# A two-block transformer with a 16,384-expert layer on one core: low halves on VectorE, the query left running, a bf16 key lookup

## The chip, the core and the metric

The program runs on one core of a Trainium2 chip. That core has TensorE (PE, whose weight loads are listed as PEld), VectorE (DVE), ScalarE (ACT), GpSimd (POOL) and a queue engine SP, all of which take their instructions strictly in order and wait for each other through semaphores. The metric is the device time of one execution in microseconds, the median of several runs, lower being better. Beside the runs there is one execution taken with the hardware profiler. All times in this text are from that execution, counted from the start of its span, unless a run is named.

## The reference

Two transformer blocks run over 512 tokens of width 1024. The change touches the last part of the second one, a layer that picks 128 experts per token (8 heads with 16 each) out of 16,384 by product keys:

```python
def block(hb):                                   # 128 tokens at a time
    qry = rms_norm((hb @ w_query).reshape(128, 8, 256), query_gain)
    s1 = einsum("thd,nd->thn", qry[..., :128], sub_keys_1)
    s2 = einsum("thd,nd->thn", qry[..., 128:], sub_keys_2)
    v1, i1 = top_k(s1, 16); v2, i2 = top_k(s2, 16)
    cand_s = (v1[..., :, None] + v2[..., None, :]).reshape(128, 8, 256)
    cand_i = (i1[..., :, None] * 128 + i2[..., None, :]).reshape(128, 8, 256)
    top_s, pos = top_k(cand_s, 16)
    experts = take_along_axis(cand_i, pos, -1)
    gates = softmax(top_s, -1)
    act = gelu(einsum("thkd,td->thk", expert_down[experts], hb))
    return einsum("thk,thkd->td", gates * act, expert_up[experts])
```

## The kernel before

Tokens lie in four tiles of 128. For tiles 1 to 3 (384 tokens) the kernel computes all 16,384 experts densely, in 128 blocks of 128 experts. A *down* of one block is 24 matmuls into a tile `dn` (L394 to L396) and a GELU on ACT; an *up* is 18 matmuls (L2030 to L2032) that add into six PSUM banks. Between the two the result is multiplied by the gate of each expert and token, which is zero for experts not chosen. For tile 0 the chosen rows are fetched from HBM by indirect DMA, 128 *down* rows and then 128 *up* rows (`gather_tile`), and DVE does one multiplication of 1024 columns for each of them (`row`, L1905, and `yacc`, L1914).

Every fp32 matmul is made of three: weights are split into a high half `whi` (ACT, L318) and a *low half* `wlo` = `raw` - `whi` (L328). The splits are made per *unit* of 128x1024 weights, which is one down or one up block, and `ws_at` keeps three units in flight. Which engine makes a low half is said by `lo_pool(u)`.

The expert layer has these stages, in program order:
- the query: 16 projections on PE, for each of 8 heads a score matmul against the keys and four rounds of `top16` (pairs of token tiles) on DVE (`query_scores`);
- the table (`NPRE` = 74 downs, whose results go to HBM). Beside them DVE makes the *choice* of each tile (`choose`: order 1, 0, 2, 3), which ends with a lookup of the chosen keys by comparing, multiplying and reducing (L1863 to L1868), and for tiles 1, 2 and 3 the *build* of the gate table (`w_build`): three PE transposes of keys and gates (L1939), then 32 steps of DVE one-hots and products (L1956, L1957, L1961) with 8 small matmuls each (L1972);
- the pairs: 54 downs, each followed by the up of the block before;
- the ups: the 74 stored blocks, 75 ups in all. For each, DVE makes `acte` (L2010, L2011), ACT `chi`, DVE `clo` (L2015); then one low half and one gather row at most.

What stands where in the engines' streams is decided while the program is written out. Generators in lanes are advanced by a clock `now` that each PE group moves forward; `room(cost)` holds a generator back while the DVE load that it has been told of (`self.dve`) is ahead of that clock. The lines of the change are in `lo_pool`, `ws_lo`, `query_scores`, `choose`, `w_build` and `peer`.

Of the kernel before, what the change touches and what calls it, by code (L numbers as in the profile page):

```python
# [23 lines left out]
P = 128  # L24
# [60 lines left out]
LO_POOL = 72  # L85
# [181 lines left out]
class Emit:  # L267
# [17 lines left out]
    def ws_open(self):  # L285

        self.units = [self.a["ws"][u] for u in range(len(self.seq) // 8)]
        self.first_expert = len(self.units)
        dn = lambda b: self.a["dn"][b]
        up = lambda b: self.a["up"][b * P:(b + 1) * P]  # L290
        for b in range(NPRE):
            self.units.append(dn(b))
        for b in range(NPRE, NB):
            self.units.append(dn(b))
            if b > NPRE:
                self.units.append(up(b - 1))
# [6 lines left out]
        self.u_dma = self.u_hi = self.u_lo = 0  # L303

# [17 lines left out]
    def ws_lo(self, upto):  # L322
        while self.u_lo < min(upto, self.NU):
            u = self.u_lo
            self.ws_hi(u + 1)
            l = self.wp.tile([P, D], F32R, tag="wlo", name=self.uid("wlo"), bufs=3)
            e = self.nc.gpsimd if self.lo_pool(u) else self.nc.vector
            e.tensor_tensor(l, self.raw.pop(u), self.hi[u].bitcast(F32), op=OP.subtract)  # L328
            self.lo[u] = l
            self.u_lo += 1  # L330

    def lo_pool(self, u):

        first = self.first_expert
        return u in self.pool_units or first - 16 <= u < first + LO_POOL or u >= first + NPRE and u % 3 == 0
# [1384 lines left out]
    def query_scores(self):  # L1720

        nc, v = self.nc, self.nc.vector
        keys = self.fp.tile([P, 2, P], F32, name="keys")
# [3 lines left out]
        def score(h, qg, q):  # L1727
            yield Q_Y
            qss = self.mmt("bg", (P, TT))
            self.sumsq(qss, q, True, True)  # L1730
            yield 0.4
            r = self.fwork((P, TT), tag="qr", bufs=2)
            v.tensor_scalar(r, qss, 1.0 / 256, EPS, op0=OP.mult, op1=OP.add)
            nc.gpsimd.tensor_tensor(r, r, self.mhalf.to_broadcast([P, TT]), op=OP.pow)
            for f in range(2):
                ps = self.mmt("bg", (P, TT, P))
                for t in range(TT):
                    nc.tensor.matmul(ps[:, t], lhsT=qg[f][:, t * P:(t + 1) * P], rhs=keys[:, f], start=True, stop=True)
                yield 0.4
                w = self.fwork((P, TT, P), tag="score_r", bufs=1)  # L1740
# [6 lines left out]
                v.tensor_tensor(val, val, r[:, :, None].to_broadcast([P, TT, 16]), op=OP.mult)  # L1747

        def head(h, ps):
            qg, q = [], []  # L1750
            for f in range(2):
                a = self.fwork(tag="qs", bufs=4)
                nc.scalar.activation(a, ps[f], AF.Square)
                q.append(a)
                g = self.fwork(tag="qg", bufs=4)
                nc.scalar.activation(g, ps[f], AF.Copy, scale=self.col("pq_gain", f))
                qg.append(g)
# [17 lines left out]
        self.drain()  # L1775
# [16 lines left out]
    def choose(self, t):  # L1792
# [45 lines left out]
        def blend(o, m, other):  # L1838
            v.tensor_tensor(other, other, o, op=OP.subtract)
            v.tensor_tensor(other, other, m, op=OP.mult)  # L1840
            v.tensor_tensor(o, o, other, op=OP.add)

        shifted(a, OP.logical_shift_right, 4)
# [5 lines left out]
        blend(a, mc, pf)  # L1849
# [5 lines left out]
        v.tensor_tensor(b, b, mc, op=OP.mult)  # L1855
        for f, sel in ((0, a), (1, b)):
            ix = s16("ch_ix")
            v.tensor_copy(ix, self.idx[f][:, t].bitcast(I32))
            for h0 in range(0, H, 4):
                hs = slice(h0, h0 + 4)  # L1860
                yield from self.room(1.2)
                oh = self.fwork((P, 4, 16, 16), tag="ch_oh", bufs=1)
                v.tensor_tensor(oh, sel[:, hs, :, None].to_broadcast([P, 4, 16, 16]),  # L1863
                                self.iota[:, None, None, :16].to_broadcast([P, 4, 16, 16]), op=OP.is_equal)
                yield from self.room(1.2)
                v.tensor_tensor(oh, oh, ix[:, hs, None, :].to_broadcast([P, 4, 16, 16]), op=OP.mult)
                yield from self.room(1.2)
                v.tensor_reduce(self.key[f][:, t, hs], oh, axis=mybir.AxisListType.X, op=OP.add)  # L1868
# [61 lines left out]
    def w_build(self, t):  # L1930
# [10 lines left out]
        sel = self.fwork((P, 4, P), F16, tag="sel")  # L1941
        nc.scalar.copy(sel[:, 0:2], ps[:, 0:2])
        nc.scalar.activation(sel[:, 2], ps[:, 2], AF.Copy, scale=G_UP)
        yield 0.8
        v.scalar_tensor_tensor(sel[:, 3], ps[:, 2], G_UP, sel[:, 2], op0=OP.mult, op1=OP.subtract)
# [6 lines left out]
        for j in range(P // 4 + 1):  # L1952
            if j < P // 4:
# [6 lines left out]
                for q in range(2):  # L1960
                    v.tensor_tensor(w[j % 2][:, q], one1, at(2 + q), op=OP.mult)  # L1961
# [89 lines left out]
    def peer(self):  # L2051
        nc, v = self.nc, self.nc.vector
        self.iota = self.fp.tile([P, P], F32, name="iota")
        nc.gpsimd.iota(self.iota, pattern=[[1, P]], base=0, channel_multiplier=0, allow_small_or_imprecise_dtypes=True)
        self.iota2 = self.fp.tile([P, P, 2], F16, name="iota2")
# [6 lines left out]
        ps = self.tok_major([[q.bitcast(F32) for q, _ in self.h], [q.bitcast(F32) for _, q in self.h]], 0)  # L2062
        for b in range(2):
            c = slice(b * T, (b + 1) * T)
            nc.scalar.copy(h2[:, c], ps[b])
            v.tensor_tensor(h2[:, c], h2[:, c], ps[2 + b], op=OP.add)
        self.chosen = set()
        self.built = set()
        self.dve = self.now
        self.dumping = False  # L2070
        lane = Lane()

        self.start_lane(lane)

        def chooses():
            for i, t in enumerate(CH_ORDER):
# [4 lines left out]
        lane.append(chooses())  # L2081
        for t in range(G0, TT):
            self.bg.append(self.w_build(t))
# [5 lines left out]
        self.gather_dt = G_DT  # L2089
        self.bg2.append(gather())  # L2090

        u = self.first_expert
        self.bp = self.fp
        kept = ExitStack()
        self.stage = kept.enter_context(self.tc.tile_pool(name="kept", bufs=1)).tile([P, P, P], F32, name="stage")
        with self.phase("table", 1):
            for b in range(NPRE):
# [181 lines left out]
```

## Time and profile before

| | us |
|---|---|
| median of 3 runs (3250.32 to 3255.26) | 3254.34 |
| the profiled execution: its time | 3259.43 |
| its span, first to last instruction | 3256.7 |
| PE busy, of the span | 3079.3 (95%) |
| DVE busy | 2298.4 (71%) |
| POOL busy | 991.7 (30%) |
| low halves on DVE, 364 of them, busy | 447.1 |
| low halves on POOL, 174 of them, busy | 466.1 |

The span is what the profile's rows are counted in. The execution's own time is 2.7 us longer, for what lies around the span, and 5.1 us above the median of the runs. Busy shares are averages over stages with different limits, so the stages are to be read one by one.

### The profile page before, as it was taken

Reading aid. Unit: us, or ns where it says so; the run is one execution under the profiler, and the core shown is the slowest. Engines: PE = TensorE matmul, PEld = TensorE weight load, DVE = VectorE, ACT = ScalarE, POOL = GpSimd, SP = SyncE. Lnnn points to the kernel's source line nnn. Section 1 sums busy time; section 2 is a strip of 40 time slices with the busy share of each in tenths; the row PEclk is TensorE's granted clock in tenths of the full one; section 3 lists DMA queues with packets and bytes.
Section 4 is the critical chain, followed back from the end, with each engine's and each line's share of the span. In section 5 each row is a group of like instructions: output and inputs, shape, how many; then the busy total and the mean of one; then the engine's idle time right before and its main releaser. Section 6 shows DMA issues by size and latency. Waiting matters only on the chain. (4 is left out here: it accounts for less than half of the span.)

```text
span 3256.7 us, 43494 instructions
## 1 busy us (share of the span) xinstructions
PE 3079.3 (95%) x16261; PEld 2637.3 (81%) x16261; DVE 2298.4 (71%) x4010; ACT 1272.5 (39%) x2033; POOL 991.7 (30%) x689
## 2 busy tenths in 40 slices
PE   8999999899999999999999997887889999999998
PEld 6778888788888888888987787786879999987776
DVE  7965542677874655346555589999897888878887
ACT  4243232455553423245326432635453333333332
POOL 3510000211110100011430244354545676654443
PEclk9999999999999999999999998999989999999999
DMA  6635542312223455324000233385858888888887
GB/s 256 258 123 202 195 153 97 104 65 72 72 72 110 162 208 199 116 81 140 27 30 30 85 112 100 112 274 174 279 175 302 311 319 312 307 298 294 301 294 261
DMA packets 218676, 576.61 MB, mean 177 GB/s; under 512 B 21344, under 2 KB 89696, under 8 KB 218336
## 3 DMA queue, kind: packets, MB, share of 16 engines
q1 hardware_dynamic: 170800, 425.04, 37.6%
q0 software_dynamic: 36864, 134.23, 12.1%
q10 hardware_dynamic: 10800, 14.56, 1.2%
q8 instruction: 127, 2.08, 0.3%
q14 instruction: 85, 0.70, 0.1%
HBM read 534.03 MB, written 39.71 MB: 176 GB/s over the span
## 5 line engine op out<-in xcount | busy, mean ns | idle before, releaser
L318 ACT CAST whi<-raw 128x1024 fp32r<-128x1024 f32 x538 | 564.2, 1050 | 624.6 <-PE mm L395 216.0
L328 DVE TENSOR_TENSOR wlo<-raw,whi 128x1024 fp32r<-128x1024 f32 x364 | 447.1, 1228 | 416.3 <-ACT whi L318 416.3
L328 POOL TENSOR_TENSOR wlo<-raw,whi 128x1024 fp32r<-128x1024 f32 x174 | 466.1, 2683 | 468.6 <-ACT whi L318 427.5
L394 PE MATMUL mm<-hh,whi 128*128 128x512 f32 x1368 | 557.8, 408 | 4.5 <-ACT hh L874 3.1
L396 PE MATMUL mm<-hh,wlo 128*128 128x512 f32 x1368 | 538.8, 394 | 6.0 <-POOL wlo L328 5.3
L395 PE MATMUL mm<-hl,whi 128*128 128x512 f32 x1368 | 537.4, 393 | 2.5 <-POOL hl L877 2.5
L394 PE MATMUL dn<-hh,whi 128*128 128x384 f32 x1024 | 362.2, 354 | 4.3 <-ACT whi L318 4.3
L396 PE MATMUL dn<-hh,wlo 128*128 128x384 f32 x1024 | 352.5, 344 | 12.2 <-POOL wlo L328 12.2
L395 PE MATMUL dn<-hl,whi 128*128 128x384 f32 x1024 | 351.6, 343 | 0.0
L2031 PE MATMUL mm<-wlo,chi 128*128 128x512 f32 x768 | 306.4, 399 | 23.5 <-POOL wlo L328 23.3
L396 PEld LDWEIGHTS mm<-hh,wlo 128*128 128x128 f32 x1368 | 258.1, 189 | 66.4 <-POOL wlo L328 7.1
L2030 PE MATMUL mm<-whi,chi 128*128 128x512 f32 x768 | 303.4, 395 | 1.4 <-ACT chi L2014 1.4
L2032 PE MATMUL mm<-whi,clo 128*128 128x512 f32 x768 | 303.7, 395 | 0.0
L394 PEld LDWEIGHTS mm<-hh,whi 128*128 128x128 f32 x1368 | 258.9, 189 | 55.3 <-ACT hh L874 3.5
L395 PEld LDWEIGHTS mm<-hl,whi 128*128 128x128 f32 x1368 | 258.8, 189 | 52.3 <-POOL hl L877 2.8
L719 POOL TENSOR_TENSOR chr<-chr,mhalf 128x1 f32<-128x1 f32 x36 | 20.5, 570 | 874.5 <-DVE chr L716 874.3
L480 PE MATMUL mm<-whi,ah 128*128 128x512 f32 x544 | 219.3, 403 | 3.5 <-DVE work L925 2.0
L482 PE MATMUL mm<-whi,al 128*128 128x512 f32 x544 | 215.6, 396 | 0.0
L481 PE MATMUL mm<-wlo,ah 128*128 128x512 f32 x544 | 215.5, 396 | 0.0
L396 PEld LDWEIGHTS dn<-hh,wlo 128*128 128x128 f32 x1024 | 198.7, 194 | 13.7 <-POOL wlo L328 13.7
L1886 POOL DMA_INDIRECT row<-down,ei x128 | 167.3, 1307 | 130.4 <-DVE row L1905 99.2
L394 PEld LDWEIGHTS dn<-hh,whi 128*128 128x128 f32 x1024 | 198.9, 194 | 7.1 <-ACT whi L318 4.6
(466 smaller groups left out, 5752.9 us busy)
## 6 DMA issues: line engine op xcount, KB each, us to landing
raw<-ws SPq DMA_DIRECT2D x282, 512.0 KB, 3.3
raw<-dn SPq DMA_DIRECT2D x128, 512.0 KB, 3.9
raw<-up SPq DMA_DIRECT2D x128, 512.0 KB, 5.4
adar<-ada SPq DMA_DIRECT2D x96, 512.0 KB, 3.7
adas<-ada SPq DMA_DIRECT2D x48, 512.0 KB, 5.8
wd<-stage SPq DMA_DIRECT2D x32, 512.0 KB, 7.2
wexp<-wd SPq DMA_DIRECT2D x128, 128.0 KB, 4.9
actd<-acte ACTq DMA_DIRECT2D x74, 192.0 KB, 4.2
```

The costliest lines, as they stand in the source:

```text
L318: self.nc.scalar.copy(h, self.raw[u])
L328: e.tensor_tensor(l, self.raw.pop(u), self.hi[u].bitcast(F32), op=OP.subtract)
L394: mm(ps, lhsT=w[0], rhs=act[0], start=first, stop=False)
L395: mm(ps, lhsT=w[0], rhs=act[1], start=False, stop=False)
L396: mm(ps, lhsT=w[1], rhs=act[0], start=False, stop=last)
L480: mm(o, lhsT=a[0], rhs=wt[0], start=k == 0, stop=False)
L481: mm(o, lhsT=a[0], rhs=wt[1], start=False, stop=False)
L482: mm(o, lhsT=a[1], rhs=wt[0], start=False, stop=k == nk - 1)
L1886: nc.gpsimd.indirect_dma_start(out=r, out_offset=None, in_=self.a[src], in_offset=bass.IndirectOffsetOnAxis(ap=ei[:, s:s + 1], axis=0))
L2030: mm(ps, lhsT=a[0], rhs=w[0], start=first, stop=False)
L2031: mm(ps, lhsT=a[0], rhs=w[1], start=False, stop=False)
L2032: mm(ps, lhsT=a[1], rhs=w[0], start=False, stop=last and i == len(cs) - 1)
```

## The change

Five things, all in the expert layer:
- `lo_pool` keeps only `pool_units` on POOL. The 16 units of the query, the first 72 of the table and every third unit of the later stages go to DVE: 148 of the 174 low halves. From the first expert on each one is told to `self.dve` with 1.15.
- `query_scores` does not drain its lanes at its end. It runs in the pool of the table stage (its tiles share buffers with `cand`, `ch_oh` and `row`), and the downs follow directly. The choices wait for `scored` = 8, and the token-major copy of tile 0's input (`h2_rows`) is made behind the second down.
- The key lookup of a choice works on bf16 tiles of 16 x 16 x 8 with the heads innermost: one comparison and one product of 2048 elements, then a tree of four additions, for each of the two key halves. Before, it was two rounds of four heads, each a comparison, a product and a reduction of 1024 fp32 elements.
- In a build step the two gate parts (a high and a low fp16 half) are multiplied by one operation of 1024 elements. Before, it was two of 512.
- The room that the lookup asks for follows its new operations.

```diff
-LO_POOL = 72
+LO_DVE = 1.15
 def ws_lo(self, upto):
             e = self.nc.gpsimd if self.lo_pool(u) else self.nc.vector
             e.tensor_tensor(l, self.raw.pop(u), self.hi[u].bitcast(F32), op=OP.subtract)
+            if u >= self.first_expert:
+                self.dve = max(self.dve, self.now) + LO_DVE
 def lo_pool(self, u):
-        first = self.first_expert
-        return u in self.pool_units or first - 16 <= u < first + LO_POOL or u >= first + NPRE and u % 3 == 0
+        return u in self.pool_units
 def query_scores(self):
-        keys = self.fp.tile([P, 2, P], F32, name="keys")
+        keys = self.fwork((P, 2, P), tag="cand", bufs=1)
...
-        self.drain()
 def choose(self, t):
-        for f, sel in ((0, a), (1, b)):
-            ix = s16("ch_ix")
-            v.tensor_copy(ix, self.idx[f][:, t].bitcast(I32))
-            for h0 in range(0, H, 4):
-                hs = slice(h0, h0 + 4)
-                yield from self.room(1.2)
-                oh = self.fwork((P, 4, 16, 16), tag="ch_oh", bufs=1)
-                v.tensor_tensor(oh, sel[:, hs, :, None].to_broadcast([P, 4, 16, 16]),
-                                self.iota[:, None, None, :16].to_broadcast([P, 4, 16, 16]), op=OP.is_equal)
-                yield from self.room(1.2)
-                v.tensor_tensor(oh, oh, ix[:, hs, None, :].to_broadcast([P, 4, 16, 16]), op=OP.mult)
-                yield from self.room(1.2)
-                v.tensor_reduce(self.key[f][:, t, hs], oh, axis=mybir.AxisListType.X, op=OP.add)
+        for f in range(2):
+            ix = self.fwork((P, 16, H), BF16, tag="ch_ix", bufs=1)
+            yield from self.room(1.45)
+            v.tensor_copy(ix.rearrange("p e h -> p h e"), self.idx[f][:, t].bitcast(I32))
+            oh = self.fwork((P, 16, 16, H), BF16, tag="ch_oh", bufs=1)
+            v.tensor_tensor(oh, sel[f][:, None].to_broadcast([P, 16, 16, H]),
+                            self.iota16[:, :, None].to_broadcast([P, 16, 16, H]), op=OP.is_equal)
+            yield from self.room(1.2)
+            v.tensor_tensor(oh, oh, ix[:, :, None].to_broadcast([P, 16, 16, H]), op=OP.mult)
+            yield from self.room(1.4)
+            for n in (8, 4, 2):
+                v.tensor_tensor(oh[:, :n], oh[:, :n], oh[:, n:2 * n], op=OP.add)
+            v.tensor_tensor(self.key[f][:, t].rearrange("p h k -> p k h"), oh[:, 0], oh[:, 1], op=OP.add)
 def w_build(self, t):
-                for q in range(2):
-                    v.tensor_tensor(w[j % 2][:, q], one1, at(2 + q), op=OP.mult)
+                v.tensor_tensor(
+                    w[j % 2], one1[:, None].to_broadcast([P, 2, 2, P, 2]),
+                    gs[:, j].rearrange("p q (g u) -> p q g u", u=2)[:, :, :, None].to_broadcast([P, 2, 2, P, 2]),
+                    op=OP.mult)
 def peer(self):
-        with self.phase("query", 1):
-            self.query_scores()
...
         with self.phase("table", 1):
+            self.query_scores()
...
             for b in range(NPRE):
                 act = self.down(b, u)
                 nc.scalar.dma_start(self.actd[b], act)
                 u += 1
+                if b == 1:
+                    h2_rows()
             self.drain(self.bg, lane, self.low)
```

The first place is PE's stream at the end of the query, from its last projection matmul (`mm` from `whi` or `wlo`, 512 columns). `ones,qs` sums squares, `keys,qg` are the scores of the last head, `ident,hh` and `ident,hl` turn tile 0's input, `dn` is the first down. Before:

```order
L396 MATMUL mm_15589<-hh_14007,wlo_15474 128x512
L586 MATMUL mm_15657<-ones,qs_15648 128x1 x4
L1738 MATMUL mm_15665<-keys,qg_15650 128x128 x4
L1738 MATMUL mm_15692<-keys,qg_15654 128x128 x4
L1926 MATMUL mm_15722<-ident,hh_14007 128x128 x4
L1926 MATMUL mm_15727<-ident,hh_14007 128x128 x4
L1926 MATMUL mm_15732<-ident,hl_14008 128x128 x4
L1926 MATMUL mm_15737<-ident,hl_14008 128x128 x4
L394 MATMUL dn_15756<-hh_14007,whi_15528 128x384
```

The same place now, where the keys lie in a buffer named `cand`:

```order
L398 MATMUL mm_15582<-hh_14007,wlo_15469 128x512
L396 MATMUL dn_15648<-hh_14007,whi_15521 128x384
L397 MATMUL dn_15648<-hl_14008,whi_15521 128x384
L398 MATMUL dn_15648<-hh_14007,wlo_15534 128x384
L396 MATMUL dn_15648<-hh_14007,whi_15521 128x384
L397 MATMUL dn_15648<-hl_14008,whi_15521 128x384
L398 MATMUL dn_15648<-hh_14007,wlo_15534 128x384
L588 MATMUL mm_15657<-ones,qs_15641 128x1 x4
L396 MATMUL dn_15648<-hh_14007,whi_15521 128x384
L397 MATMUL dn_15648<-hl_14008,whi_15521 128x384
L398 MATMUL dn_15648<-hh_14007,wlo_15534 128x384
L1740 MATMUL mm_15668<-cand_14737,qg_15642 128x128 x4
```

Downs now stand in front of the last head's scores and between them.

The second place is PE's stream in the third build, between two of its 32 steps (`mm` from `work` and `x`; each of its eight matmuls has a weight load ahead of it). Before:

```order
L1972 MATMUL mm_19283<-work_19182,x_19184 128x128
L394 MATMUL dn_19271<-hh_14007,whi_19198 128x384
L395 MATMUL dn_19271<-hl_14008,whi_19198 128x384
L396 MATMUL dn_19271<-hh_14007,wlo_19210 128x384
L394 MATMUL dn_19271<-hh_14007,whi_19198 128x384
L395 MATMUL dn_19271<-hl_14008,whi_19198 128x384
L396 MATMUL dn_19271<-hh_14007,wlo_19210 128x384
L1972 LDWEIGHTS x_19184
L1972 MATMUL mm_19307<-work_19183,x_19184 128x128
```

The same place now:

```order
L1976 MATMUL mm_19726<-work_19716,x_19718 128x128
L1976 LDWEIGHTS x_19718
L1976 MATMUL mm_19738<-work_19717,x_19718 128x128
L1976 LDWEIGHTS x_19718
L1976 MATMUL mm_19738<-work_19717,x_19718 128x128
```

Not one down is left between the steps of this build. Counted over the stage: from the transposes of the first build to those of the third there were 1128 down matmuls and are now 1485; behind the latter there were 477 and are now 57. The first build's transposes stood behind 219 down matmuls and stand behind 282.

The third place is DVE's stream in the ups, three blocks (`raw`, `whi` and `wlo` are a unit's weights, `row` a gathered row). Before:

```order
L2015 TENSOR_TENSOR clo_24602<-acte_24497,chi_24601 128x384
L1914 SCALAR_TENSOR_TENSOR yacc_22617<-row_24488,gact,yacc_22617 128x1024
L328 TENSOR_TENSOR wlo_24623<-raw_24551,whi_24615 128x1024
L2010 TENSOR_TENSOR acte_24534<-acte_24534,wexp_24536 128x256
L2011 TENSOR_TENSOR acte_24534<-acte_24534,stage 128x128
L2015 TENSOR_TENSOR clo_24639<-acte_24534,chi_24638 128x384
...
L1914 SCALAR_TENSOR_TENSOR yacc_22617<-row_24575,gact,yacc_22617 128x1024
L2010 TENSOR_TENSOR acte_24605<-acte_24605,wexp_24607 128x256
L2011 TENSOR_TENSOR acte_24605<-acte_24605,stage 128x128
L2015 TENSOR_TENSOR clo_24713<-acte_24605,chi_24712 128x384
```

And now:

```order
L2019 TENSOR_TENSOR clo_24616<-acte_24511,chi_24615 128x384
L1914 SCALAR_TENSOR_TENSOR yacc_22354<-row_24499,gact,yacc_22354 128x1024
L329 TENSOR_TENSOR wlo_24637<-raw_24565,whi_24629 128x1024
L2014 TENSOR_TENSOR acte_24548<-acte_24548,wexp_24550 128x256
L2015 TENSOR_TENSOR acte_24548<-acte_24548,stage 128x128
L2019 TENSOR_TENSOR clo_24653<-acte_24548,chi_24652 128x384
L1914 SCALAR_TENSOR_TENSOR yacc_22354<-row_24539,gact,yacc_22354 128x1024
L329 TENSOR_TENSOR wlo_24674<-raw_24602,whi_24666 128x1024
L2014 TENSOR_TENSOR acte_24585<-acte_24585,wexp_24587 128x256
L2015 TENSOR_TENSOR acte_24585<-acte_24585,stage 128x128
L2019 TENSOR_TENSOR clo_24690<-acte_24585,chi_24689 128x384
```

Of the 74 blocks of the ups, DVE's stream had 24 with a `yacc` and then a `wlo`, 21 with a `wlo` and then a `yacc`, 23 with a `yacc` alone (the low half being on POOL), 4 with a `wlo` alone and 2 with neither. It now has 35, 28, 0, 10 and 1.

## Rows read from the trace of the kernel before

**Rows 1.** Windows by stage: length, busy and instructions per engine, clock, DMA share, GB/s.

```profile
1976.00:2031.00 55.00, 41.38 (x224) 40.45 (x222) 53.42 (x154) 18.93 (x24) 25.97 (x10) 0.89 0.40 128
2031.00:2188.00 157.00, 133.62 (x874) 124.98 (x874) 152.92 (x357) 76.86 (x90) 67.60 (x32) 0.95 0.57 185
2188.00:2339.00 151.00, 115.58 (x772) 104.63 (x772) 148.16 (x280) 70.69 (x81) 82.53 (x44) 0.94 0.69 224
2339.00:2464.00 125.00, 111.94 (x734) 103.66 (x735) 100.61 (x178) 62.01 (x73) 54.00 (x34) 0.91 0.63 209
2464.00:2899.00 435.00, 435.00 (x2187) 392.89 (x2187) 363.95 (x454) 156.89 (x209) 299.59 (x177) 1.00 0.88 311
2899.00:3250.00 351.00, 326.08 (x1375) 255.11 (x1374) 282.54 (x355) 111.41 (x152) 153.02 (x92) 1.00 0.85 288
```

**Rows 2.** Timeline of PE at the query's last projection and behind it.

```profile
1965.58 0.40 PE L396 MATMUL mm<-hh,wlo 128*128 128x512 f32 x1
1968.68 1.87 PE L586 MATMUL mm<-ones,qs 128*128 128x1 f32 x8 [2.70 <-DVE qs L1758]
```

**Rows 3.** Timeline of PE at the first and at the third build's transposes.

```profile
2022.53 0.34 PE L396 MATMUL dn<-hh,wlo 128*128 128x384 f32 x1
2022.70 0.34 PE L394 MATMUL dn<-hh,whi 128*128 128x384 f32 x1
...
2031.58 0.48 PE L1939 MATMUL mm<-ident,key 128*128 128x128 f32 x1 [8.09 <-DVE key L1868]
...
2039.81 0.82 PE L1972 MATMUL mm<-work,x 128*128 128x128 f16 x8
...
2339.27 0.47 PE L1939 MATMUL mm<-ident,key 128*128 128x128 f32 x1 [8.75 <-DVE key L1868]
```

**Rows 4.** Groups of DVE by form, table: busy us, mean ns, idle before.

```profile
L1961 DVE TENSOR_TENSOR work<-one,sel 128x512 f16<-128x512 f16 x192 | 106.6, 596 | 0.0
L1956 DVE TENSOR_TENSOR one<-iota,sel 128x512 f16<-128x512 f16 x96 | 73.7, 768 | 2.4
```

**Rows 5.** The build's tiles on DVE, table: duration min/median/max in ns.

```profile
L1961 DVE TENSOR_TENSOR work<-one,sel x192: 409/418/3221, 2039.3 to 2439.2; 128x512 f16<-128x512 f16 x192
L1956 DVE TENSOR_TENSOR one<-iota,sel x96: 401/425/3164, 2038.6 to 2438.2; 128x512 f16<-128x512 f16 x96
```

**Rows 6.** Timeline of DVE in the first choice's lookup.

```profile
2011.20 1.22 DVE L1863 TENSOR_TENSOR ch_oh<-ch_a,iota 128x1024 f32<-128x1024 f32 x1
2012.45 1.23 DVE L1866 TENSOR_TENSOR ch_oh<-ch_oh,ch_ix 128x1024 f32<-128x1024 f32 x1
...
2017.06 3.31 DVE L1866 TENSOR_TENSOR ch_oh<-ch_oh,ch_ix 128x1024 f32<-128x1024 f32 x1
```

**Rows 7.** Timeline of POOL in the same stretch.

```profile
2016.66 2.63 POOL L328 TENSOR_TENSOR wlo<-raw,whi 128x1024 fp32r<-128x1024 f32 x1 [0.71 <-ACT whi L318]
```

**Rows 8.** Timeline of DVE over three blocks of the ups.

```profile
3043.41 0.56 DVE L2015 TENSOR_TENSOR clo<-acte,chi 128x384 fp32r<-128x384 f32 x1 [0.71 <-ACT chi L2014]
...
3045.09 1.22 DVE L328 TENSOR_TENSOR wlo<-raw,whi 128x1024 fp32r<-128x1024 f32 x1
3046.22 0.42 DVE L2010 TENSOR_TENSOR acte<-acte,wexp 128x256 f32<-128x256 f32 x1
...
3047.55 0.56 DVE L2015 TENSOR_TENSOR clo<-acte,chi 128x384 fp32r<-128x384 f32 x1 [0.71 <-ACT chi L2014]
...
3052.76 0.56 DVE L2015 TENSOR_TENSOR clo<-acte,chi 128x384 fp32r<-128x384 f32 x1 [0.71 <-ACT chi L2014]
3057.39 0.56 DVE L2015 TENSOR_TENSOR clo<-acte,chi 128x384 fp32r<-128x384 f32 x1 [0.71 <-ACT chi L2014]
```

**Rows 9.** Timeline of PE in the ups.

```profile
3054.28 0.40 PE L2030 MATMUL mm<-whi,chi 128*128 128x512 f32 x1
3054.52 0.39 PE L2031 MATMUL mm<-wlo,chi 128*128 128x512 f32 x1
```

**Rows 10.** Waits in the ups, 2899 to 3250: total us, times, longest.

```profile
PE mm L2031 <- POOL wlo L328: 23.3, 22, 2.5
```

More of the change, by code (lines that the diff above doesn't have):

```diff
@@ L1747, in score @@
                 v.tensor_tensor(val, val, r[:, :, None].to_broadcast([P, TT, 16]), op=OP.mult)
+            self.scored += 1
         def head(h, ps):
-            qg, q = [], []
+            q, qg = (self.bp.tile([P, 2, T], F32, tag="row", name=self.uid(n), bufs=4) for n in ("qs", "qg"))
+            q, qg = ([t[:, f] for f in range(2)] for t in (q, qg))
             for f in range(2):
[L1752 to L1757, printed above, removed]
+                nc.scalar.activation(q[f], ps[f], AF.Square)
+                nc.scalar.activation(qg[f], ps[f], AF.Copy, scale=self.col("pq_gain", f))
             v.tensor_tensor(q[0], q[0], q[1], op=OP.add)
@@ L1836, in shifted, with blend @@
             v.tensor_copy(o, ti)
-        def blend(o, m, other):
+        def blend(o, m, other, to=None):
             v.tensor_tensor(other, other, o, op=OP.subtract)
             v.tensor_tensor(other, other, m, op=OP.mult)
-            v.tensor_tensor(o, o, other, op=OP.add)
+            v.tensor_tensor(o if to is None else to.rearrange("p s h -> p h s"), o, other, op=OP.add)
+        sel = [self.fwork((P, 16, H), BF16, tag="ch_s%d" % f, bufs=1) for f in range(2)]
         shifted(a, OP.logical_shift_right, 4)
@@ L2054, in peer @@
         nc.gpsimd.iota(self.iota, pattern=[[1, P]], base=0, channel_multiplier=0, allow_small_or_imprecise_dtypes=True)
+        self.iota16 = self.fp.tile([P, 16, 8], BF16, name="iota16")
+        v.tensor_copy(self.iota16, self.iota[:, :16, None].to_broadcast([P, 16, 8]))
         self.iota2 = self.fp.tile([P, P, 2], F16, name="iota2")
@@ L2058, in peer @@
         self.actd = self.dp.tile([NPRE, P, TD], F32, name="actd")
-        with self.phase("query", 1):
-            self.query_scores()
+        self.bp = self.fp
         h2 = self.fwork((P, D), tag="h2", bufs=1)
[L2062 to L2066, printed above, removed]
         self.chosen = set()
         self.built = set()
+        self.scored = 0
         self.dve = self.now
         self.dumping = False
-        lane = Lane()
-        self.start_lane(lane)
+        kept = ExitStack()
+        self.stage = kept.enter_context(self.tc.tile_pool(name="kept", bufs=1)).tile([P, P, P], F32, name="stage")
         def chooses():
+            while self.scored < 8:
+                yield 0.2
+            self.dve = max(self.dve, self.now)
             for i, t in enumerate(CH_ORDER):
@@ L2088, in gather @@
             yield from self.gather_tile(0, h2)
-        self.gather_dt = G_DT
-        self.bg2.append(gather())
         u = self.first_expert
-        self.bp = self.fp
-        kept = ExitStack()
-        self.stage = kept.enter_context(self.tc.tile_pool(name="kept", bufs=1)).tile([P, P, P], F32, name="stage")
         with self.phase("table", 1):
+            self.query_scores()
+            lane = Lane()
+            self.start_lane(lane)
+            lane.append(chooses())
+            for t in range(G0, TT):
+                self.bg.append(self.w_build(t))
+            self.gather_dt = G_DT
+            self.bg2.append(gather())
             for b in range(NPRE):
```

26 lines of the change are left out of this document (16 added, 10 removed).

## The prediction

> **What bounds the kernel now.** I read the windows by stage first, then TensorE's (PE's) timeline at the joints of the stages, then VectorE's (DVE's) groups and timelines. In the pairs PE is busy for all of 435 us at full clock [rows 1]; nothing but less PE work shortens that stage, and the change leaves PE's work as it is. In the table DVE is the busy engine: 53.4 of 55 us, 152.9 of 157, 148.2 of 151, and only then 100.6 of 125, while PE has gaps [rows 1]. In the ups neither is full, but PE loses 23.3 us waiting for low halves that POOL makes [rows 10].
>
> Why is DVE so full in the table? The build's product takes 418 ns in the median and 596 in the mean, its one-hot 425 and 768, with maxima over 3 us [rows 4, 5]. A pair in the lookup shows where this comes from: the same multiplication takes 1.23 us, and 3.31 when POOL's subtraction runs from 2016.66 for 2.63 us [rows 6, 7]. So a low half on POOL is not free for DVE. Two groups alone pay 192 x 0.178 + 96 x 0.343 = 67 us, for 72 subtractions by POOL in the table: at least 0.93 us each. The single case of 3.31 gives 2.08 as the other end. On DVE itself the subtraction takes 1.13 between starts [rows 8]. Moving it costs DVE between 0.2 us and nothing, or gives back up to 0.95.
>
> **The unit costs.** A down matmul starts every 0.173 us (2022.53 to 2022.70 and its neighbours) [rows 3], an up matmul every 0.235 [rows 9]. A build's 256 small matmuls take PE about 17 us (an estimate: eight, with what follows them, hold it for 0.5). A build step on DVE is a one-hot, a second like it and two products, each 0.34 apart when undisturbed (the 0.42 of [rows 5] less the overlap of about 0.08 that 1.22 against 1.13 shows [rows 8]): 1.36.
>
> No bf16 lookup is in the trace. fp16 operations of 512 take 418 ns and an fp32 operation of 256 takes 0.42 [rows 5, 8], so 16-bit pairs go two to a step. If bf16 does the same, a comparison of 2048 costs what one of 1024 fp32 costs, 1.25 with its wait [rows 6], the product too, the four additions 0.69 + 0.42 + 0.28 + 0.29 = 1.7 and the cast 0.2: 4.4 per key half. Before it was two rounds of three operations at 1.25 and a cast, 7.65. That saves 3.25 per half, 6.5 per choice. At one element per step it would be 7.4 and save nothing. I take two per step, as the fp16 rows do. The merged gate product is 0.61 for 0.68, which saves 2 us per build: small.
>
> **The table, in three pieces.** *From the last projection (1965.6) to the first build's transposes (2031.6): 66.0 now* [rows 2, 3]. PE has 282 down matmuls there, 49 us, and waits for DVE in the end, as it does now (8.09). DVE's chain decides: the last head's scores, the choice, the lookup. The lookup ran from 2011.2 to 2031.6, 20.4 us with its stretches, and should take 8.8: -11.6. Twelve low halves join it: 12 x 1.13 = +13.6. Ten subtractions by POOL go; what they stretched outside the lookup I put at 8 us (between 0 and 10 x 2.08 less the 5 in the lookup, so 16). Sum 66 - 11.6 + 13.6 - 8 = 60. That the downs no longer wait for the last head's scores (the 2.70 us wait and what follows it [rows 2]) doesn't shorten this chain; it gives PE work that it would have to do later.
>
> *From there to the third build's transposes (2339.3): 307.7 now.* PE had 1128 down matmuls there and now has 1485: 257 us, two builds 34, so 291 at least. DVE was busy for 301 of 308. It loses the stretch of 48 subtractions (45 at 0.93 to 100 at 2.08), loses three lookups' savings (19) and 4 for the products, and gains 62 low halves (70) and 12 more gathered rows at 1.13 (14): 262 to 317. Two engines that both need nearly 300 and wait for each other in every step of a build don't overlap fully; I take 312, near DVE's upper end. So this piece is 4 us longer, and holds 357 more downs.
>
> *From there to the first up (2464.2): 124.9 now, with 477 downs beside the build; now 57.* The third build stands almost alone. From the transposes to its first matmul it was 8.2 us in the first build (2031.58 to 2039.81) [rows 3]. Then 32 steps at 1.31 = 42 us, 13 gathered rows between them 15, and 48 downs behind them 8.3: 73. So 52 less.
>
> Together 60 + 312 + 73 = 445 for 498.6: **53.6 us less**. In substance: downs that were late have been moved to where PE stood idle.
>
> **The pairs.** PE's 54 downs and 53 ups stay, 435 us. DVE gets 35 more low halves. Its longest common sequence is now three gathered rows, two low halves and the gate work, which is 4.14 less one row and one low half, 1.8 [rows 8]: 3 x 1.2 + 2 x 1.13 + 1.8 = 7.7. PE's pair is 435 / 53 = 8.2. What hides DVE is PE, with half a microsecond to spare; from there on, all would show. I take 0.
>
> **The ups.** A block costs PE 18 x 0.235 = 4.2. DVE's cycle from `clo` to `clo` is 4.14 with the gathered row ahead of the low half, 5.21 where POOL subtracts beside it, 4.63 where the low half stands directly behind `clo` [rows 8]. Now the 5.21 are gone: 35 blocks at 4.14, 28 at 4.63, 10 without a gathered row at about 3.4, which is 309 us, under PE's 75 x 4.2 = 317. The runs of 4.63 lag by 0.4 a block, six in a row, and three units in flight cover that. So PE no longer waits for POOL: the 23.3 us [rows 10] go, and small follow-on gaps with them; I take 351 - 25 = 326 (bounds 317 and 345). The last unit's wait of 2.5 is among them.
>
> [...]
>
> **Sum.** 53.6 + 25 = 79 us less. Against the profiled execution, 3259.4 - 79 = 3180; that execution lies 5.1 above the median of the runs, which would become 3175. **I say 3177.**
>
> **Rivals.**
> - *PE decides the middle piece* (the stretches were near 2 us each, DVE drops out): 291 instead of 312, the ups at 317: 3177 - 30 = 3147. For it: 3.31 against 1.23 [rows 6]. Against: builds couple the engines. Chance 0.10. [...]
> - *bf16 goes one element per step*: 6.5 us more in the first choice, which is all on the chain, and 19 in three others, of which perhaps two thirds show: 3196. For it: no bf16 row. Against: fp16. Chance 0.10.
> - *DVE becomes the bound in the pairs*: a wait of 0.4 for `whi` in front of both low halves (what 4.63 has over the same work in 4.14 [rows 8]) makes 7.7 into 8.5, and 53 x 0.3 = +16, 3193; with a late row besides, twice that. Against it: DVE was busy for 364 of 435 us with the stretches in it [rows 1]. Chance 0.10.
> - *The freed time is not found*: the builds keep taking what they took although POOL is silent, since the coupling and not the stretch cost it, 35 us in the two middle builds: 3212. Chance 0.10.
> - *Slower*: the stretches are not POOL's subtractions' doing (DMA or fetches would do as well). Then DVE gets 72 low halves in the table for nothing, 81 us, less 26 for lookups, on an engine that is full for 460 of 488, +55; in the ups every third cycle of 5.21 becomes 6.3, 25 x 1.1 = +28; together 3254 + 83 = 3337. It decides where a POOL subtraction costs DVE under about 0.4 us. Against it: the two rows side by side [rows 6, 7] and an undisturbed median [rows 5]. Chance 0.05.
>
> That leaves 0.55 for the forecast, whose own range is 3160 to 3195. From these: faster by over 0.2% (which is about what a measurement of this kernel can tell from none) 0.94, the same 0.02, slower 0.04. The range that leaves out the slow case and the halves of the outermost two is 3150 to 3215.
>
> **What would show it.** Right: product and one-hot means at their medians of 0.42; the first build's transposes at 2020 to 2033, the third's within 15 us of 2338, the first up at 2400 to 2425; pairs 435 at full PE; no wait of PE for POOL in the ups, and some 326 us there. Lookup operations of 2048 at 1.2 us (2.2 would be one element per step). After the third build a stretch of some 60 us in which PE does little; if the granted clock falls there (0.91 in that stage now [rows 1]), the 48 downs behind it take up to 8 us more. Wrong: gaps of PE in the pairs, `wlo` waits that now name DVE, or a DVE that is still 97% busy with its medians unchanged.

## The result and the profile after

The median is 3159.8 us (3153.8 to 3163.6, four runs) against 3252.9 for the kernel before (one run more than in the table above): a ratio of 0.9712, interval 0.9694 to 0.9730. The prediction was 3177, its range 3150 to 3215. Unless a run is named, everything below is from the profiled execution, which took 3161.1 us with a span of 3159.4.

First the page of the kernel after: busy time of each engine, and the slices of PE and of the clock that was granted to it.

```profile
PE 3057.0 (97%) x16261; PEld 2628.7 (83%) x16261; DVE 2191.7 (69%) x4063; ACT 1270.8 (40%) x2033; POOL 622.8 (20%) x541
...
PE   8999999999999999999999999999969999999999
...
PEclk9999999999999999999999999999968999999999
```

DVE is busy for 107 us less although it makes 148 more low halves. The one slice in which PE and the clock both show a 6 is the third build. The windows by stage answer to [rows 1] (same columns). The boundaries are the same events: the first down, the transposes of the three builds, the first up, the last down and the end of the ups.

```profile
1961.50:2019.00 57.50, 55.61 (x327) 55.21 (x326) 53.68 (x220) 24.23 (x31) 1.86 (x1) 0.97 0.44 144
2019.00:2168.50 149.50, 147.22 (x1005) 141.19 (x1004) 136.67 (x354) 84.79 (x102) 15.37 (x12) 1.00 0.72 240
2168.50:2314.00 145.50, 145.50 (x1000) 140.26 (x999) 134.07 (x290) 82.85 (x98) 36.27 (x28) 1.00 0.91 295
2314.00:2392.00 78.00, 45.32 (x319) 37.21 (x319) 65.95 (x135) 37.76 (x40) 14.90 (x16) 0.58 0.56 174
2392.00:2826.50 434.50, 434.50 (x2185) 392.39 (x2184) 348.76 (x481) 156.99 (x209) 201.91 (x142) 1.00 0.87 311
2826.50:3154.00 327.50, 324.30 (x1378) 255.89 (x1376) 253.53 (x376) 110.76 (x152) 85.41 (x60) 1.00 0.89 299
```

In the second and third line, which hold the first two builds, the roles have changed: PE is busy for 292.7 of 295 us and DVE for 270.7, where DVE was the full one. In the fourth line PE is idle for 33 of 78 us and its mean granted clock is 0.58.

PE's timeline at the joints, to be held against [rows 2, 3]: the last query projection, the transposes of the first and third build, the third build's first and last steps, and the downs behind it.

```profile
1961.48 0.39 PE L398 MATMUL mm<-hh,wlo 128*128 128x512 f32 x1
2018.77 0.38 PE L1939 MATMUL mm<-ident,key 128*128 128x128 f32 x2
2314.16 0.38 PE L1939 MATMUL mm<-ident,key 128*128 128x128 f32 x2
2320.84 0.63 PE L1976 MATMUL mm<-work,x 128*128 128x128 f16 x8 [4.62 <-DVE work L1962]
2380.38 1.03 PE L1976 MATMUL mm<-work,x 128*128 128x128 f16 x8 [1.44 <-DVE work L1962]
2381.64 0.52 PE L397 MATMUL dn<-hl,whi 128*128 128x384 f32 x1
```

The 8.09 and 8.75 us that PE waited for keys in front of two builds are gone. DVE's groups by form in the table, answering to [rows 4, 6]:

```profile
L1962 DVE TENSOR_TENSOR work<-one,gsel 128x1024 f16<-128x1024 f16 x96 | 65.6, 684 | 0.0
L1958 DVE TENSOR_TENSOR one<-iota,sel 128x512 f16<-128x512 f16 x96 | 40.6, 423 | 2.1
L1861 DVE TENSOR_TENSOR ch_oh<-ch_s,iota 128x2048 bf16<-128x2048 bf16 x8 | 10.8, 1349 | 0.0
L1864 DVE TENSOR_TENSOR ch_oh<-ch_oh,ch_ix 128x2048 bf16<-128x2048 bf16 x8 | 9.8, 1221 | 0.1
```

The one-hot's mean fell from 768 ns to its undisturbed 423. The bf16 operations of 2048 elements take 1.35 and 1.22 us, about what the fp32 ones of 1024 took (1.22 and 1.23), so bf16 does go two elements to a step here. Last, all waits of PE's matmuls in the ups, where 23.3 us for POOL stood [rows 10], and the longest wait of its weight loads (PEld) there:

```profile
PE mm L2035 <- DVE wlo L329: 1.8, 11, 0.2
PE mm L2034 <- ACT chi L2018: 1.2, 1, 1.2
...
PEld mm L2035 <- DVE wlo L329: 8.8, 17, 0.6
```

| us | before | predicted | after |
|---|---|---|---|
| last projection to first build | 66.0 | 60 | 57.3 |
| to third build | 307.7 | 312 | 295.4 |
| to first up | 124.9 | 73 | 77.7 |
| pairs | 434.5 | 435 | 434.5 |
| ups, to the last matmul | 351.5 | 326 | 327.3 |

### The profile page after: what moved, and what is told of

It is laid out like the page before. It is cut to its first block, busy times and chain, and to the rows that moved or that the text cites. A ratio compares the mean times of both kernels' runs of the same rounds, so it can differ in the third digit from the quotient of the medians.

```text
span 3159.4 us, 43356 instructions
## 1 busy us (share of the span) xinstructions
PE 3057.0 (97%) x16261; PEld 2628.7 (83%) x16261; DVE 2191.7 (69%) x4063; ACT 1270.8 (40%) x2033; POOL 622.8 (20%) x541
## 3 DMA queue, kind: packets, MB, share of 16 engines
q8 instruction: 127, 2.08, 0.3%
## 4 chain that ended last, share of the span: by engine, by line
PE 79%; DVE 13%; issue 3%; ACT 3%; DMA 2%; POOL 1%; SPq 0%; ACTq 0%; DVEq 0%; POOLq 0%
PE mm L396 9%; PE mm L397 8%; PE mm L398 8%; PE dn L396 5%; PE dn L398 5%; PE dn L397 5%; PE mm L482 4%; PE mm L483 4%; PE mm L484 4%; PE mm L2035 4%; PE mm L2036 4%; PE mm L2034 4%; PE mm L1208 2%; DVE adas L625 2%; DVE wlo L329 2%
## 5 line engine op out<-in xcount | busy, mean ns | idle before, releaser
L329 DVE TENSOR_TENSOR wlo<-raw,whi 128x1024 fp32r<-128x1024 f32 x512 | 627.9, 1227 | 434.1 <-ACT whi L319 433.2
L396 PE MATMUL dn<-hh,whi 128*128 128x384 f32 x1024 | 352.0, 344 | 0.0
L398 PE MATMUL dn<-hh,wlo 128*128 128x384 f32 x1024 | 345.7, 338 | 2.2 <-DVE wlo L329 2.2
L1886 POOL DMA_INDIRECT row<-up,ei x128 | 181.4, 1417 | 304.8 <-DVE yacc L1914 285.8
L397 PEld LDWEIGHTS dn<-hl,whi 128*128 128x128 f32 x1024 | 193.8, 189 | 2.2
```

What stands on the lines that cost most here:

```text
L396: mm(ps, lhsT=w[0], rhs=act[0], start=first, stop=False)
L397: mm(ps, lhsT=w[0], rhs=act[1], start=False, stop=False)
L398: mm(ps, lhsT=w[1], rhs=act[0], start=False, stop=last)
L1886: nc.gpsimd.indirect_dma_start(out=r, out_offset=None, in_=self.a[src], in_offset=bass.IndirectOffsetOnAxis(ap=ei[:, s:s + 1], axis=0))
```

## The experiments

The theory: a POOL subtraction of some 2.7 us holds DVE up by 0.9 to 2 us, so moving it to DVE frees DVE; that lets builds and downs overlap, and PE decides the table. The planner is the code that sets the order of the streams; `LO_DVE` is the DVE time in us that it counts for one low half. Rivals: the gain comes from where the downs now stand (the planner is told 1.15 for each low half); it comes from the lookup and the undrained query; the stretches have another cause. Ratios are to the kernel before in the same session; one thousandth is 3.25 us.

### Who makes the low halves, and what the planner is told

Three runs complete a two-by-two table with the kernel after.

```diff
 # e1_pool_told and e3_pool_untold: the old rule, back on POOL
-        return u in self.pool_units
+        first = self.first_expert
+        return u in self.pool_units or first - 16 <= u < first + LO_POOL or u >= first + NPRE and u % 3 == 0
 # e2_dve_untold and e3_pool_untold: told nothing
-LO_DVE = 1.15
+LO_DVE = 0.0
```

> The kernel after with the low halves back on GpSimd as before (148 units), while the planner is still told 1.15 for each, so every down, build step and lookup stands where it stands after. It changes who does the work and nothing else. My theory (a GpSimd subtraction stretches VectorE's two-input operations by 0.9 to 2 us): VectorE wins nothing, product and one-hot means go above their medians again, PE waits for GpSimd's low halves again (some 12 us in the table, some 20 in the ups); 3185 to 3225 us, ups 345 to 351. Rival (GpSimd's work is free for VectorE, the gain came from where the downs stand): VectorE loses 1.13 x 120 of busy time, means at medians; 3150 to 3165.

> The kernel after with the planner told nothing of the low halves (0 in place of 1.15); they stay on VectorE. By the written order the first and third builds' transposes then stand behind 234 and 1206 down matmuls (282 and 1767 after), and 201 stand behind the third build's last step (48 after). If the placing of the downs is a cause of its own: the middle piece is set by VectorE at 270 to 290 us with PE waiting for its products, the last piece is 100 to 125 instead of 78; together 440 to 470 for 430, so 3170 to 3200 us. If the placing doesn't matter and only VectorE's freedom counts: 3155 to 3165. Pairs and ups stay at 434.5 and 327 by both.

> Both undone: low halves on GpSimd as before, and the planner told nothing (234, 1206 and 201 as in the run with 0); the query left running, the bf16 lookup and the merged product stay. What is left of the gain is theirs. My theory: lookups (26 us of VectorE in the table, about 12 in the first piece) and products (6), with the stretches back: 3215 to 3235 us. Rival (the gain came mostly from the lookup and the undrained query): 3160 to 3185.

| median us (ratio, interval) | told 1.15 | told nothing |
|---|---|---|
| low halves on DVE | after: 3159.8 (0.9712, 0.9694 to 0.9730) | 3167.6 (0.9739, 0.9723 to 0.9755) |
| low halves on POOL | 3222.4 (0.9901, 0.9885 to 0.9918) | 3240.1 (0.9954, 0.9937 to 0.9970) |

Down a column only the engine differs, and every down, build step and lookup stands in the same place: 61 us told (0.0189), 70 us untold (0.0215). Along a row only the places differ: 9 us on DVE, 17 on POOL. What neither factor touches (query, lookup, product) is worth 15 us in the lower right corner. So the engine is the main cause and the placing a smaller one. The run with both undone came out 5 us above its range. In e1_pool_told the time is inside its range (3185 to 3225), but the ups took 343.4 us, just under the 345 to 351 expected, and PE waits for POOL's low halves for 5.5 us in the table and 14.1 in the ups, less than the 12 and 20 expected. The table grew by 43 us, and its line shows DVE 53 us busier than the 390.4 of after:

```profile
1965.00:2438.00 473.00, 404.88 (x2643) 380.62 (x2642) 443.60 (x925) 229.75 (x271) 243.60 (x127) 0.91 0.66 212
```

PE's matmuls of the table, as many as after, took 404.9 us instead of 393.7. The piece with the first two builds alone has 14 us more of it: PE has gaps there now, and its mean granted clock is 0.96, against 1.00 after. So beside its waits PE also lost time to its clock.

In e1_pool_told one choice shows the stretch in undiluted form. DVE's timeline, and POOL's in the same stretch:

```profile
2011.89 3.31 DVE L1866 TENSOR_TENSOR ch_oh<-ch_oh,ch_ix 128x2048 bf16<-128x2048 bf16 x1
2015.23 3.57 DVE L1869 TENSOR_TENSOR ch_oh<-ch_oh 128x1024 bf16<-128x1024 bf16 x3
2020.61 3.25 DVE L1866 TENSOR_TENSOR ch_oh<-ch_oh,ch_ix 128x2048 bf16<-128x2048 bf16 x1
2023.89 1.48 DVE L1869 TENSOR_TENSOR ch_oh<-ch_oh 128x1024 bf16<-128x1024 bf16 x3
```

```profile
2011.31 2.80 POOL L330 TENSOR_TENSOR wlo<-raw,whi 128x1024 fp32r<-128x1024 f32 x1 [1.67 <-ACT whi L320]
2015.47 2.72 POOL L330 TENSOR_TENSOR wlo<-raw,whi 128x1024 fp32r<-128x1024 f32 x1 [1.36 <-ACT whi L320]
2019.63 3.15 POOL L330 TENSOR_TENSOR wlo<-raw,whi 128x1024 fp32r<-128x1024 f32 x1 [1.44 <-ACT whi L320]
```

The same product that takes 1.22 after takes 3.31 and 3.25 beside a subtraction, and ends about 1.1 us after POOL's does, nearly its own length. DVE's busy time in this run is 2272.1, that is 80.4 above after, with 148 low halves fewer at 1.13: the price of one subtraction is (80.4 + 148 x 1.13) / 148 = 1.67 us on the mean. The same sum by stage gives 0.5 in the query's projections, 2.1 in the piece with the first two builds, 1.6 in the pairs and 2.0 in the ups: what a subtraction costs depends on what DVE does beside it.

With nothing told, 3167.6 lies between what the two theories gave, and the table did not behave as either said: it takes 427.2 us, not 440 to 470, and no more than after (430.4). The loss is in the ups, 332.8 where 327 was expected, and behind them. DVE's timeline of e2_dve_untold at the end shows a part of it:

```profile
3148.82 2.60 DVE L1914 SCALAR_TENSOR_TENSOR yacc<-row,gact,yacc 128x1024 f32<-128x1024 f32 x2
3151.53 0.69 DVE L2051 TENSOR_TENSOR work<-yacc,grow 128x512 f32<-128x512 f32 x1
```

Gathered rows run until 3151.4, and tile 0's output only then begins; after has its last row at 3119.7. The planner, told less, puts fewer rows into the table (44 against 51), and the rest run late. Inside the ups another thing fits: 37 blocks instead of 28 have the low half directly ahead of the row, an order whose cycle is 4.62 us (the last experiments below come back to it). No run takes these two apart at 0.

### Work on POOL that nobody uses

`twin(u)` names the first 72 units of the table and every third of the later stages, 133 in all. The results go nowhere. To make room for the scratch tile, two pairs of the choice's small tiles share a buffer, which these lines do not show.

```diff
             e.tensor_tensor(l, self.raw.pop(u), self.hi[u].bitcast(F32), op=OP.subtract)
+            if self.twin(u):
+                s = self.fwork(dt=BF16, tag="twin")
+                for h in (self.hi[u][:, :T].bitcast(F32), self.hi[u][:, T:].bitcast(F32)):
+                    self.nc.gpsimd.tensor_tensor(s, h, h, op=OP.subtract)
```

> The kernel after, every low half on VectorE and every down where it stands after, plus work that nobody uses: for 133 units (72 of the table, every third later) GpSimd subtracts the unit's high half from itself in two operations of 512 columns into a bf16 scratch tile. (Two pairs of the choice's small tiles share a buffer to make room.) VectorE's own work is unchanged, so its busy time shows the stretch alone. My theory: 0.9 to 2 us more of VectorE busy for each unit, 120 to 265 us in all; where PE and VectorE are both full it shows in the time: 3195 to 3260 us. Rival (something else stretched them, DMA or fetches): busy time and means as after, 3155 to 3170.

It took 3290.0 us (1.0111, 1.0094 to 1.0128): 130 us slower than after, slower even than before, and beyond the 3260 that I gave. DVE's line of the page in this run, its low halves and build products in the table, and PE's longest wait there and in the ups:

```profile
PE 3095.6 (94%) x16261; PEld 2639.0 (80%) x16261; DVE 2384.7 (73%) x4063; ACT 1267.0 (39%) x2033; POOL 1018.4 (31%) x807
```

```profile
L330 DVE TENSOR_TENSOR wlo<-raw,whi 128x1024 fp32r<-128x1024 f32 x76 | 111.1, 1461 | 3.9 <-ACT whi L320 3.8
L1973 DVE TENSOR_TENSOR work<-one,gsel 128x1024 f16<-128x1024 f16 x96 | 79.0, 823 | 0.0
```

```profile
PE mm L1987 <- DVE work L1973: 56.0, 54, 3.6
...
PE mm L2046 <- DVE wlo L330: 26.2, 50, 1.4
```

DVE's instructions are as many as after (4063), and its busy time is 193 us more: 1.45 for each unit. This settles the cause of the stretches: apart from the shared buffers, only POOL's work was added, and the build products, which do not touch those buffers, went from 684 to 823 ns. The time grew by more than I allowed because DVE's work became late for PE in every stage: 73 us in the table, 5 in the pairs, 45 in the ups. The first two builds again ran at a lower mean clock, 0.96, and their matmuls took 21 us longer.

### The parts one at a time

```diff
 # e4_drain: at the end of query_scores
+        self.drain()
 # e6_twomul: in w_build
+                for q in range(2):
+                    v.tensor_tensor(w[j % 2][:, q], one1, gs[:, j, q].rearrange("p (g u) -> p g u", u=2)[:, :, None, :].to_broadcast([P, 2, P, 2]), op=OP.mult)
 # e5_lookup32: the fp32 lookup of before, with its rooms, in the kernel after (lines as in the change above)
 # e8_low_only: the kernel before, with
-        return u in self.pool_units or first - 16 <= u < first + LO_POOL or u >= first + NPRE and u % 3 == 0
+        return u in self.pool_units
+            if u >= self.first_expert:
+                self.dve = max(self.dve, self.now) + LO_DVE
```

> The kernel after with the lanes drained again at the end of the query, as before; the rest as after. By the written order 234 downs instead of 282 stand ahead of the first build's transposes, 1485 in the middle as after, and 57 more in the third build. If the drain costs what it takes from PE at its place: PE idles some 8 us more behind the last projection, has 8.3 us less of downs to do, and the 57 go where PE stands idle anyway in the third build: 3158 to 3168 us. Rival (the query left running is a main part of the gain): 3175 to 3190.

> The kernel after with the gate parts multiplied by two operations of 512 again; every down and every planner figure as after. The busy means are 684 ns for one of 1024 and 418 for one of 512, but ends overlap: I sized it at 2 us per build, of which only the third build's shows, since PE decides the other two: 3158 to 3165. Rival (a second operation has a cost of its own in each of 96 steps, 0.15 us): some 5 us in the third build, 3163 to 3170.

> The kernel after with the fp32 lookup of before (two rounds of compare, multiply, reduce for each key half, with the rooms of before); it moves downs too: the transposes of the builds stand behind 336, 1266 and 1776 (282, 1029 and 1767 after). By my sum VectorE has 6.5 us more in each choice: the first piece is some 6 to 9 us longer, the middle is set by PE and hides the others: 3165 to 3175. Rival (the lookup is a main part of the gain, VectorE decides the table): 26 us, 3183 to 3195. Rival (bf16 goes one element per step, nothing saved): 3155 to 3163.

> The kernel before with one part of the change alone: low halves on VectorE and told with 1.15 each; query drained, fp32 lookup, two products as before. The transposes of the builds stand behind 288, 1218 and 1776 downs. After the run with low halves on GpSimd and untold came out 12 us under before, what remains for this part is some 80 us if parts add: 3170 to 3185 us, ups 327, no wait of PE for GpSimd. If VectorE decides the table once the lookup is slow again, 3185 to 3200. If the low halves only pay together with a lighter lookup: above 3210.

| | median us | ratio (interval) |
|---|---|---|
| e4_drain | 3160.6 | 0.9716 (0.9695 to 0.9736) |
| e6_twomul | 3161.1 | 0.9713 (0.9694 to 0.9731) |
| e5_lookup32 | 3179.3 | 0.9770 (0.9752 to 0.9788) |
| e8_low_only | 3184.4 | 0.9782 (0.9761 to 0.9803) |

Draining the query costs nothing measurable, nor does the second product. The low halves alone, moved and told, give 71 us of the 94; that run is in its range, with ups of 327 and no wait of PE for POOL there. The old lookup costs 19 us, more than the 5 to 15 that I expected and short of the 23 to 35 of the rival in which DVE decides the table. Its place is seen in PE's waits of e5_lookup32 behind the first build's transposes:

```profile
PE mm L1938 <- DVE ch_ix L1857: 20.4, 1, 20.4
PE mm L1938 <- DVE key L1867: 8.0, 1, 8.0
```

I had taken the later lookups as hidden under PE. But with the old rooms the written order puts 1776 of the 1824 down matmuls ahead of the third build, so PE runs out of them and stands for 28 us in front of the third build's transposes while DVE finishes that choice. The piece between first and third transposes took 313.6 us (295.4 after), the first piece 66.6 (57.3): these 9.3 us are just above the 6 to 9 expected for the first lookup, and they also hold three more low halves (14 instead of 11). So the lookup's own part was not measured alone: this run moves downs too.

### Cover for the third build

The downs missing beside the third build can be brought back by telling the planner less. A second constant turned out to matter in the ups.

```diff
-LO_DVE = 1.15
+LO_DVE = 0.85      # c1_lo85, c2_lo85_rows;  0.6 in c3_lo60_rows
-G_DT3 = 4.2
+G_DT3 = 3.9        # c2_lo85_rows, c3_lo60_rows, c4_rows
```

> The kernel after with the planner told 0.85 for a low half in place of 1.15. The transposes then stand behind 273, 900 and 1527 downs (282, 1029, 1767 after; 234, 756, 1206 with 0), 48 behind the third build as after: 249 downs stand inside the third build in place of 9. If PE decides the first two pieces after and VectorE the third, the middle loses 231 downs x 0.173 = 40 us down to what VectorE needs there (258 to 265 of 295), and the third piece takes the 240 downs into its idle time and grows by 5 to 15: the table is 402 to 415 for 430, 3133 to 3148 us. If the placing is neutral, as the table's 427 with 0 might say: 3155 to 3165. The last gathered row stands one block before the end (7 after), so the end may show it: plus 2.

> The run with 0.85, and the gathered rows of the ups paced at 3.9 in place of 4.2, so that the last stands 6 blocks before the end. If the last rows show in the end of the run with 0.85, this is 1 to 5 us faster than it; if not, the same within 2.

> The planner told 0.6 for a low half, rows of the ups at 3.9: transposes behind 258, 852 and 1425 downs, 351 inside the third build, 48 behind it. Middle 1167 downs: PE 236, VectorE some 250; third piece 399 downs: PE 86 with the build. If both engines can be full there, the table is 400 to 410: 3130 to 3143 us. If they wait for each other in each step (as with 0, where PE and VectorE were both idle a tenth of the middle), 415 to 425: 3145 to 3158.

> The kernel after (1.15 told) with the gathered rows of the ups paced at 3.9 in place of 4.2, and nothing else. At 0.85 this pace gave 10 us (3157 to 3147), 9 of them in the ups (329 to 320). If the pace works on every block (a row in each block in place of two patterns, VectorE waiting 13.4 us less for high halves), the ups fall from 327 to 320 and the time to 3150 to 3154. If it only repaired the late last row of the run with 0.85 (here the last row is 34 us ahead of the last up already): 3157 to 3162.

| | told, row pace | median us | ratio (interval) | table | ups |
|---|---|---|---|---|---|
| after | 1.15, 4.2 | 3159.8 | 0.9712 (0.9694 to 0.9730) | 430.4 | 327.3 |
| c1_lo85 | 0.85, 4.2 | 3157.0 | 0.9697 (0.9684 to 0.9711) | 425.1 | 328.7 |
| c2_lo85_rows | 0.85, 3.9 | 3147.0 | 0.9667 (0.9654 to 0.9680) | 422.2 | 319.8 |
| c3_lo60_rows | 0.6, 3.9 | 3142.3 | 0.9648 (0.9631 to 0.9664) | 415.4 | 320.5 |
| c4_rows | 1.15, 3.9 | 3156.2 | 0.9697 (0.9684 to 0.9710) | 428.9 | 320.7 |

c3_lo60_rows beats both kernels, at the slow edge of what I gave (3130 to 3143); but its table, 415.4, is that of the other case, in which the engines wait for each other (415 to 425). With 0.85 alone the table gained 5 us where I expected 15 to 28, and its time, 3157.0, is in the range that I gave for a neutral placing (3155 to 3165). The middle came out near the 258 to 265 expected (266.5), the third piece did not: 102.8 for 83 to 93. DVE's timeline at the start of the third build of c1_lo85 shows a wait that I had left out:

```profile
2302.51 1.23 DVE L329 TENSOR_TENSOR wlo<-raw,whi 128x1024 fp32r<-128x1024 f32 x1 [4.17 <-ACT whi L319]
2307.88 1.23 DVE L329 TENSOR_TENSOR wlo<-raw,whi 128x1024 fp32r<-128x1024 f32 x1 [4.14 <-ACT whi L319]
2309.03 0.42 DVE L1958 TENSOR_TENSOR one<-iota,sel 128x512 f16<-128x512 f16 x1
```

A low half on DVE waits for its high half on ACT, and the build steps behind it in the same queue wait with it: 16.5 us in six waits. The high halves were late in their turn; one reason is that ACT waited for weights that had not landed yet:

```profile
ACT whi L319 <- DMA raw<-dn: 11.9, 5, 3.9
```

How much of the third piece this decides stays open; no run here isolates it.

The row pace gave 10 us at 0.85 where 1 to 5 were expected, so it does more than mend the end. In the kernel after 28 blocks of the ups have the low half directly behind `clo`, where it waits 0.40 us for `whi`, and their cycle is 4.62 us; PE's 18 matmuls take 4.20. In c4_rows 63 blocks have the row first, with a cycle of 4.14 in the median, none has the other order, and PE's weight loads wait 0.3 us for low halves instead of 8.8. In the profile its ups fall by 7 us, as expected. The time does not confirm as much: 3156.2 is outside both ranges that I gave (3150 to 3154 and 3157 to 3162), between the medians of after and c4_rows lie 3.6 us, and their intervals overlap. Only at 0.85 is the pace's gain clear of the noise.

## Why the prediction was right, point by point

- **POOL's subtraction costs DVE more than moving it.** Right in kind, mis-sized: I gave 0.93 to 2.08 and worked near 0.93, "between 0.2 us and nothing, or gives back up to 0.95". It is 1.67 on the mean in e1_pool_told (for two half-width operations of e7_twin together 1.45), and 2.1 in the piece with the first two builds, the upper end of what I gave. Dividing two groups' stretch by all 72 subtractions had given only a lower bound, as I said, and I then leaned on it. Moving one gives DVE 0.54 back (80.4 / 148).
- **The middle piece, 312.** This is the step that was off, by 17 us. It followed from the low price: "near DVE's upper end". DVE was busy for 271 us, near the 262 that the sum gives with the high price, and PE decides: its 291 became 293 busy and 2.2 of waits, together 295. So the part of the first rival that concerns the middle piece, which I had given 0.10, came true. In e1_pool_told a subtraction of some 2.7 us cost DVE about 2.1 in this piece. The other part of that rival, ups at 317, did not come about: they took 327. "Builds couple the engines" held no more once DVE had room.
- **The first piece, 60**: 57.3. The lookup's half took 4.53 us between starts (2004.48 to 2009.01) where I worked out 4.4.
- **The third piece, 73**: 77.7. The build stands alone as said, 59.5 us from first to last step. A step without a row took 1.40 us where I had worked out 1.31, which is 3 us over the 32. The granted clock was 0.50 between 2325 and 2381, where PE was busy for 29.4 of 56 us in short pieces; the 15 down matmuls that still ran at that clock, most of them 0.32 us apart in place of 0.17, lost 2.3 us, within the 8 that I had allowed.
- **Pairs, 0**: 434.5, and PE waited for nothing. **Ups, 326**: 327.3, without a wait for POOL; what is left over PE's 75 x 4.2 = 315 is in part the 8.8 us that its weight loads waited for DVE's low halves, although I had written that "three units in flight cover that".
- **The rival "slower"** needed a price under 0.4 us; it is four times that. "The freed time is not found" fell with the means at their medians, and bf16 at one element per step fell with 1.22 us for 2048.
- **What I could not see**: the query ended 4.1 us earlier. In the profiles of the runs whose kernels are the same up to there, the last projection matmul starts anywhere from 1959.6 to 1965.5, so a difference of this size is within the scatter between executions. The stages together gave 92.4 us for a predicted 79: 16.6 more from the middle piece and 2.7 from the first, less 4.7 in the third and 1.3 in the ups. That these smaller misses partly cancel is luck.

## What to carry to other kernels

Work given to POOL was not free for DVE here: a subtraction of some 2.7 us on POOL cost DVE 1.67 on the mean (e1_pool_told) and 1.13 when DVE made it itself, so moving it paid even in the table, where DVE was the full engine. To find such a cost, compare means with medians of DVE's operations, and look beside the outliers on POOL's timeline. For another operation the two numbers have to be measured again, in the stage that counts: by stage the price went from 0.5 to 2.1. When the bound moves to another engine, look where its work has gone: here the downs that filled PE were missing beside the third build, and telling the planner a smaller cost for each low half brought another 14 us (c4_rows to c3_lo60_rows).

## What the runs showed of the hardware

Not every DVE operation is held. In e1_pool_told 22 MAX8, 30 FIND_INDEX8 and 11 MATCH_REPLACE8 of 88 columns lie wholly inside a POOL subtraction, and none took over 251 ns; some operations of 128 columns that else take 0.29 us or less took up to 2.7. DVE's tiles in that run, minimum, median and maximum:

```profile
L1783 DVE MAX8 top<-cand x32: 227/233/253, 1985.0 to 2326.4; 128x8 f32<-128x88 f32 x32
...
L1841 DVE TENSOR_TENSOR ch_pf<-ch_pf,ch_mc x4: 291/293/2722, 2002.6 to 2340.1; 128x128 f32<-128x128 f32 x4
L1856 DVE TENSOR_SCALAR ch_mc<-ch_mc x4: 219/1324/2428, 2007.3 to 2348.7; 128x128 f32<-128x128 f32 x4
```

In the kernel before, eight TENSOR_REDUCE of 1024 elements lie wholly inside a subtraction as well, at 1.22 us at most, so the old lookup's reductions went undisturbed there, and the additions of the new one do not (3.57 against 1.48 above). In the rows of e1_pool_told the two-input `ch_pf` was held (2722 against 293 ns), and so was the TENSOR_SCALAR `ch_mc`, which reads one tile (2428 against 219). What sets these apart from the MAX8 and the reductions no run here shows.
